# A hybrid decoder trunk on one core: loads of the attention stage issued in smaller pieces and in slots of their own

## The chip, the cores and the metric

The kernel runs on one core of a Trainium2 chip. The metric is the device time of one execution in microseconds (us), taken over several runs; lower is better.

## The reference

Two residual layers over 2048 tokens of width 1024, in float32. The first layer is gated linear attention, the second a dilated sliding-window attention, and both carry a small cross-attention into a memory. The change lies in the second layer:

```python
DIL_GROUPS = ((128, 1), (512, 4), (2048, 16))      # window, dilation
for g, (window, dil) in enumerate(DIL_GROUPS):
    base = g * 3 * MIXER_WIDTH
    qkv = (h @ w_in[:, base:base + 3 * MIXER_WIDTH]).reshape(B, T, 3, DIL_HEADS, DIL_HEAD_DIM)
    q = partial_rope(qkv[:, :, 0], pos)
    k = partial_rope(qkv[:, :, 1], pos)
    o, lse = dilated_group(q, k, qkv[:, :, 2], window, dil)     # blocks of 128 queries, 256 keys
    outs.append(o); lses.append(lse)
wts = jax.nn.softmax(jnp.stack(lses, axis=0), axis=0)
o = jnp.einsum('gbth,gbthd->bthd', wts, jnp.stack(outs, axis=0))
...
branch = jnp.concatenate([o, mem_o], axis=-1) * jax.nn.silu(gate)
x = x + branch @ w_out[i]
```

Six heads of width 128 are computed once for each of three groups. Each head's three outputs are then mixed with softmax weights from the three log-sums, and multiplied by the gate.

## The kernel before

TensorE works in float16 halves: each product is three matmuls (`mm3`, lines 180 to 182: high by high, high by low, low by high).

**The units stage.** `heads` lists 18 units, six heads by the groups 2, 1, 0. The loop at line 1374 runs over 144 slots, `s = 8 n + e`, eight for each unit. A slot does, in this order: the scores of slot s - 10 (`att_scores`), the P·V of slot s - 13 (`att_pv`), and one projection of 512 tokens (`proj_t`): q in even slots, k in odd ones, of the present unit. So a unit's q and k are made while the unit before is still being scored.

- After each q and k pair `evac` (L1171 to L1175) empties PSUM. After every second pair `rope_quad` rotates the first 32 rows: a shuffle (L1181), a product on GpSimd (L1182), a product and a sum on VectorE (L1183, L1184), split halves (L1187 on ScalarE, L1188 on VectorE), and eight copies back into q and k (L1193). The second rotation is wanted by the first scores of its unit.
- `att_scores`: masks and maxima on VectorE (L1223), the statistics (L1227), exponentials on ScalarE (L1232), halves on ScalarE and GpSimd (L173, L174: `ph`), and a DMA transpose from SP (L175: `pt<-ph`) that `att_pv` reads three slots later. `att_pv` copies four blocks of output into `osb`, which goes to memory (`od`).
- `pair_raw` loads a unit's weights, two pieces for q and two for k of 256 KB each, into the one buffer `stg`; `pair_norm` and `pair_split` (L829) scale and split them. `load_v` loads a unit's values, 1 MB, into one of two buffers.
- When a head's three groups are done (x = 0 in the count `h, x = divmod(s - 35, 24)`), `prep_load` loads the log-sums (`nm`, `dn`), and `prep_mix` makes the mixing factors and stores them (`fd<-nm`). Then four quarters y follow, one mix each: `item_og` loads the gate `sg` and three outputs `og`, `item_fb` loads the factors `fb`, spread to all partitions, and `item_mix` forms two products on GpSimd (L1339, L1344), one on VectorE (L1341), two sums (L1347, L1348) and the product with the gate (L1350), and stores it (L1352, `brd<-sg`). `sg`, `og` and `fb` have one buffer each, so a quarter's loads wait for the mix before it. Five heads pass this way in the stage; the sixth is mixed in the tail.

**What sets the order.** Only TensorE runs in program order (`manual_schedule` for PE). The other engines and SP, which issues all DMAs, are ordered by the scheduler when the kernel is built: it places an instruction by its own idea of when its inputs are ready, so program order is a priority and not a slot. At run time each engine then works through its own list strictly in order.

Of the kernel before, what the change touches and what calls it, by code (L numbers as in the profile page):

```python
# [7 lines left out]
F32 = mybir.dt.float32  # L8
F32R = mybir.dt.float32r
F16 = mybir.dt.float16  # L10
# [6 lines left out]
P = 128  # L17
T = 2048
D = 1024
KT = 8  # L20
# [15 lines left out]
def trunk(ctx, tc, a, out):  # L36
    nc = tc.nc
    PE, V, A, G, SY = nc.tensor, nc.vector, nc.scalar, nc.gpsimd, nc.sync
    uid = [0]

    def tl(pool, shape, dt, tag):
        uid[0] += 1
        return pool.tile(shape, dt, name=f"{tag}_{uid[0]}", tag=tag)

    def pool(name, bufs=1, side="left", space=None):
        kw = {"space": space} if space is not None else {"side": side}
        return tc.tile_pool(name=name, bufs=bufs, **kw)
# [10 lines left out]
    stg = ctx.enter_context(pool("stg", 1))  # L58
# [19 lines left out]
    def col(n=1):  # L78
        ncol[0] += n
        return cols[:, ncol[0] - n:ncol[0]]  # L80
# [231 lines left out]
    def neg_of(inv):  # L312
        t = col()
        V.tensor_scalar(out=t, in0=inv, scalar1=-1.0, scalar2=None, op0=ALU.mult)
        return t

    x, w_in_a, w_in_b = a["x"], a["w_in_a"], a["w_in_b"]
# [9 lines left out]
    v_d = {(hp, g, i): tl(dram, [P, 4, 2, 4, P], F16, f"vd{hp}_{g}_{i}") for hp in range(3) for g in range(3)  # L327
           for i in range(2)}
# [26 lines left out]
    with ExitStack() as c1:  # L355
        k1 = c1.enter_context(pool("k1", 2, "right"))
        k2 = c1.enter_context(pool("k2", 1, "right"))
        k0 = c1.enter_context(pool("k0", 1, "right"))
# [223 lines left out]
        for b in range(NB):  # L582
# [28 lines left out]
            if 2 <= b < 7:  # L611
                c0 = 1552 if b == 2 else 1808 + (b - 3) * 256
# [164 lines left out]
    def gdst(t, g, c):  # L777
        if g == 0:
            return t[:, c * 512:(c + 1) * 512]
        f = GROUPS[g][0]  # L780
        n = 512 // f
        return t.rearrange("p (f l) -> p f l", f=f)[:, :, c * n:(c + 1) * n]
# [5 lines left out]
    def wbase(u):  # L788
        return u[1] * 2304 + u[0] * 256

    def pair_raw(c0s):
        raw = tl(stg, [P, KT, 256], F32, "stg")
        for j, c0 in enumerate(c0s):
            v = w_in_b[:, c0:c0 + P].rearrange("(k p) n -> p k n", p=P)
            for k0 in (0, 4):
                SY.dma_start(raw[:, k0:k0 + 4, j * P:(j + 1) * P], v[:, k0:k0 + 4, :])
        return dict(raw=raw, w=[], m=len(c0s))

    def pair_norm(d, cps, common=False):
        raw = d["raw"]  # L800
# [25 lines left out]
    def pair_split(d, j):  # L826
        w, r = d["w"][j], d["raw"][:, :, j * P:(j + 1) * P]
        A.activation(out=w[:, 0], in_=r, func=AF.Copy, scale=d["s"][j])
        V.scalar_tensor_tensor(out=w[:, 1], in0=r, scalar=d["s"][j], in1=w[:, 0], op0=ALU.mult, op1=ALU.subtract)  # L829

    def proj_t(w, c):
        t = mm_bank()
        cs = slice(c * 512, (c + 1) * 512)
        for k in range(KT):
            mm3(t, w[:, 0, k], w[:, 1, k], h2T[:, 0, k, cs], h2T[:, 1, k, cs], k == 0, k == KT - 1)
        return t
# [4 lines left out]
    def head_cols(n):  # L841
        if n == len(heads):
            return GATE2[1:]
        u, i = heads[n]
        return [wbase(u) + i * P, wbase(u) + 768 + i * P]

    with ExitStack() as cv:
# [203 lines left out]
        def memq(c):  # L1051
            for pr in range(2):
                out_q(c, pr, proj_t(wq["w"][pr], c))

        wq = pair_raw([6912, 7040])
        pair_norm(wq, ps_g, True)
        for j in range(2):
# [100 lines left out]
    vp = c4.enter_context(pool("vp", 2))  # L1158
    bk = c4.enter_context(pool("bk", 1))
    qp = c4.enter_context(pool("qp", 2))  # L1160

    def load_v(n):
        u, i = heads[n]
        vt = tl(vp, [P, 4, 2, 4, P], F16, "v")
        SY.dma_start(vt, v_d[u[0], u[1], i])
        return vt

    def evac(ts, c, g, dsts, X):
        r0 = 64 * (c // 2)
        for j in range(2):  # L1170
            A.activation(out=X[r0 + 32 * j:r0 + 32 * j + 32, :], in_=ts[j][0:32, :], func=AF.Copy)  # L1171
        for j in range(2):
            hi = gdst(dsts[j][:, 0, :], g, c)
            A.activation(out=hi, in_=perm(ts[j], g), func=AF.Copy, scale=SQ)
            V.scalar_tensor_tensor(out=gdst(dsts[j][:, 1, :], g, c), in0=perm(ts[j], g), scalar=SQ, in1=hi,  # L1175
                                   op0=ALU.mult, op1=ALU.subtract)

    def rope_quad(c, g, dsts, X):
        cs = slice(c * 512, (c + 1) * 512)
        W = tl(bk, [P, 512], F32, "rw")  # L1180
        V.stream_shuffle(W, X, SWAP)  # L1181
        G.tensor_tensor(out=W, in0=W, in1=rope[1][:, cs], op=ALU.mult)  # L1182
        V.tensor_tensor(out=X, in0=X, in1=rope[0][:, cs], op=ALU.mult)  # L1183
        V.tensor_tensor(out=W, in0=X, in1=W, op=ALU.add)  # L1184
        hl = X.bitcast(F16).rearrange("p (a n) -> p a n", a=2)
        hi, lo = fold(hl[:, 0], g), fold(hl[:, 1], g)
        A.activation(out=hi, in_=perm(W, g), func=AF.Copy, scale=SQ)  # L1187
        V.scalar_tensor_tensor(out=lo, in0=perm(W, g), scalar=SQ, in1=hi, op0=ALU.mult, op1=ALU.subtract)  # L1188
        for y in range(2):
            for j in range(2):  # L1190
                r0 = 64 * y + 32 * j
                for x in range(2):
                    V.tensor_copy(gdst(dsts[j][0:32, x, :], g, c + 2 * y), fold(hl[r0:r0 + 32, x], g))  # L1193
# [124 lines left out]
    def item_og(h, c, osb=None):  # L1318
        cs = slice(c * 512, (c + 1) * 512)
        sg = tl(bk, [P, 512], F32, "sg")  # L1320
        SY.dma_start(sg, sg_d[h][:, cs])
        og = tl(gk, [P, 3, 512], F32, "og")
        if h < 5:
            SY.dma_start(og[:, 0, :], o_d[h][0][:, cs])
        SY.dma_start(og[:, 1, :].rearrange("p (f l) -> p f l", f=4), gdst(o_d[h][1], 1, c))
        SY.dma_start(og[:, 2, :].rearrange("p (f l) -> p f l", f=16), gdst(o_d[h][2], 2, c))
        return h, c, sg, og

    def item_fb(h, c):
        fb = tl(gk, [P, 3, 16, 32], F32, "fb")  # L1330
        src = f_d[h][c, 0, :]
        SY.dma_start(fb.rearrange("p g q l -> p (g q l)"),
                     bass.AP(tensor=src.tensor, offset=src.offset, ap=[[0, P], [1, 1536]]))
        return fb
# [22 lines left out]
    hds, live = {}, {}  # L1357
    wcur, wnext = cur, nxt
# [6 lines left out]
    def scores(at):  # L1365
        att_scores(hds[at // 8], at % 8)

    def pv(at):
        att_pv(hds[at // 8], at % 8)
        if at % 8 == 7 and at // 8 % 3 < 2:  # L1370
            att_stats(hds.pop(at // 8), 0)

    preps, items = {}, {}
    for s in range(NS):
        n, e = divmod(s, 8)
        if s >= 10:
            scores(s - 10)
        if s >= 13:
            pv(s - 13)
        u, i = heads[n]  # L1380
        if e == 0:
            d = wcur
            sc = col()
            V.tensor_scalar(out=sc, in0=d["inv"][0], scalar1=d["inv"][1],
                            scalar2=(128.0 ** -0.5) / (SQ * SQ), op0=ALU.mult, op1=ALU.mult)
            hds[n] = dict(u=u, h=u[0] * 2 + i, sc=sc, nsc=neg_of(sc), pv={}, st={}, osb={},
                          ns=16 if n + 1 < NH else 4, qk=[tl(qp, [P, 2, T], F16, nm) for nm in ("q", "k")])
            if n > 0:
                wnext = pair_raw(head_cols(n + 1))
        c = (0, 2, 1, 3)[e // 2]  # L1390
        live[e % 2] = proj_t(d["w"][e % 2], c)
        if e % 4 == 0:
            rx = tl(bk, [P, 512], F32, "rx")
        if e % 2 == 1:
            evac([live[0], live[1]], c, u[1], hds[n]["qk"], rx)
            wcur = wnext
        if e % 4 == 3:
            rope_quad(c % 2, u[1], hds[n]["qk"], rx)
        if e == 2:
            pair_norm(wcur, ps_tr)  # L1400
        elif 4 <= e < 4 + wcur["m"]:
            pair_split(wcur, e - 4)
        if e == 6:
            hds[n]["v"] = load_v(n)
        h, x = divmod(s - 35, 24)
        if 0 <= h < 5:
            step = 4 if h < 4 else 2
            if x == 0:
                att_stats(hds[3 * h + 2], 0)
                preps[h] = prep_load(h)  # L1410
            if x == 1:
                prep_mix(preps.pop(h))
            y, z = divmod(x - 3 - step, step)
            if 0 <= y < 4 and z == 0:
                item_mix(*items.pop(y))
            y, z = divmod(x - 1 - step, step)
            if 0 <= y < 4 and z == 0:
                items[y] = (item_og(h, y), item_fb(h, y))

    WSH = [P, 4, 256]  # L1420

# [32 lines left out]
    for x in range(14):  # L1454
# [114 lines left out]
        if x in (7, 8, 9, 10):  # L1569
            j, kh = divmod(x - 7, 2)  # L1570
# [9 lines left out]
    for p_ in range(NB):  # L1580
        d = fs.pop(p_)
# [69 lines left out]
```

## Time and profile before

| | |
|---|---|
| runs, median of 3 | 2658.17 us (2656.22 to 2658.51) |
| the profiled execution, its time | 2655.69 us |
| its span, first to last instruction | 2653.7 us |
| mean granted TensorE clock | 0.982 |
| busy: PE, DVE, ACT, POOL | 95%, 61%, 51%, 21% of the span |
| DMA queue of SP | 346.84 MB, 47.6% of 16 engines |

In the profile PE is TensorE, DVE VectorE, ACT ScalarE, POOL GpSimd, SP the queue that issues DMAs. `ps_g` are the banks of scores, `ps_o` and `ps_tr` those of P·V, `ps_mm` and `ps_x` those of projections. A row of a timeline has the start in us, the duration, engine, line, operation, output and inputs, and in brackets how long the engine stood idle before it and what ended that. A transfer in the chain is timed from its issue to its landing. Buffer numbers are left out there, and kept in the orders below.

### The profile page before, as it was taken

The page shows a single profiled execution, that of the slowest core. Times are in us where ns is not written, and L with a number is a line of the kernel's source. Part 1 is how long each engine was busy: PE and PEld are TensorE (multiplying, and loading weights), DVE is VectorE, ACT ScalarE, POOL GpSimd, SP SyncE. Part 2 cuts the span into 40 slices and gives each one's busy share as a digit, 9 for nine tenths or more (in the row PEclk, how much of TensorE's full clock was granted, in tenths as well). Part 3 has the DMA queues.
Part 4 walks back from the last instruction along what each step waited for, and adds up shares of the span by engine and source line. Part 5 has one row for each costly group of instructions (what it writes and reads, how often), then busy time and mean ns, then how long its engine had stood idle before and what let it go on. Part 6 is the DMA issues. An engine that isn't in the chain of part 4 may idle for free.

```text
span 2653.7 us, 45228 instructions
## 1 busy us (share of the span) xinstructions
PE 2524.5 (95%) x17137; PEld 1696.6 (64%) x17137; DVE 1607.6 (61%) x3595; ACT 1343.0 (51%) x2957; POOL 565.5 (21%) x471
## 2 busy tenths in 40 slices
PE   7989999899999999999999999999899998988899
PEld 6879999788889644444444455445454554545798
DVE  7445544656865756556546555766857767577742
ACT  6355544635444446656546455455454554546322
POOL 0000000001211224555442122222322223232200
PEclk9999999999999999999999999999999998999999
DMA  6232111333433445667674244564745547458652
GB/s 207 82 126 98 62 57 70 124 106 104 147 95 95 143 161 138 168 161 187 163 183 143 59 87 104 143 159 108 183 101 146 157 107 184 100 141 216 198 170 87
DMA packets 528493, 349.72 MB, mean 132 GB/s; under 512 B 355650, under 2 KB 467732, under 8 KB 525588
## 3 DMA queue, kind: packets, MB, share of 16 engines
q1 hardware_dynamic: 528276, 346.84, 47.6%
q8 instruction: 134, 2.20, 0.4%
q14 instruction: 83, 0.68, 0.1%
HBM read 185.74 MB, written 95.86 MB: 106 GB/s over the span
## 4 chain that ended last, share of the span: by engine, by line
PE 69%; DMA 9%; DVE 9%; issue 5%; ACT 4%; POOL 2%; SPq 2%; DVEq 0%; ACTq 0%; POOLq 0%
PE ps_mm L180 13%; PE ps_mm L181 13%; PE ps_mm L182 13%; PE ps_x L181 5%; PE ps_x L182 5%; PE ps_x L180 5%; DMA fb<-fd 2%; DMA pt<-ph 1%; PE ps_tr L167 1%; PE ps_o L180 1%; PE ps_o L182 1%; PE ps_o L181 1%; DMA stg<-in_w_in_b 1%; PE ps_g L180 1%; PE ps_g L554 1%
## 5 line engine op out<-in xcount | busy, mean ns | idle before, releaser
L180 PE MATMUL ps_mm<-h2T,w 128*128 128x512 f16 x1112 | 427.3, 384 | 1.8 <-ACT c L947 1.8
L181 PE MATMUL ps_mm<-h2T,w 128*128 128x512 f16 x1112 | 426.4, 383 | 0.0
L182 PE MATMUL ps_mm<-h2T,w 128*128 128x512 f16 x1112 | 425.5, 383 | 0.0
L180 PE MATMUL ps_mm<-w,hT 128*128 128x256 f16 (+1 forms) x1408 | 388.0, 276 | 4.3 <-ACT v L490 1.3
L181 PE MATMUL ps_mm<-w,hT 128*128 128x256 f16 (+1 forms) x1408 | 386.7, 275 | 0.0
L182 PE MATMUL ps_mm<-w,hT 128*128 128x256 f16 (+1 forms) x1408 | 385.5, 275 | 0.4 <-DVE hT L384 0.4
L182 PEld LDWEIGHTS <-w 128*128 128x128 f16 x1952 | 192.3, 99 | 236.1 <-issue 9.1
L181 PEld LDWEIGHTS <-w 128*128 128x128 f16 x1952 | 192.4, 99 | 221.4 <-issue 14.9
L180 PEld LDWEIGHTS <-w 128*128 128x128 f16 x1952 | 192.6, 99 | 214.2 <-issue 7.1
L174 POOL TENSOR_TENSOR ph<-pm,ph 128x512 f16<-128x512 f32 (+2 forms) x144 | 147.2, 1022 | 613.3 <-ACT ph L173 449.3
L1232 ACT ACTIVATE pm<-pm,st,cols 128x256 f32<-128x256 f32 (+1 forms) x288 | 156.4, 544 | 167.1 <-DVE st L1227 166.0
L180 PE MATMUL ps_x<-h2T,w 128*128 128x512 f16 x552 | 210.3, 381 | 3.4 <-ACT h2T L701 2.0
L181 PE MATMUL ps_x<-h2T,w 128*128 128x512 f16 x552 | 210.4, 381 | 1.4 <-DVE h2T L702 1.4
L182 PE MATMUL ps_x<-h2T,w 128*128 128x512 f16 x552 | 210.1, 381 | 0.0
L174 POOL TENSOR_TENSOR stg<-mp,stg 128x512 f16<-128x512 f32 x16 | 18.6, 1159 | 751.7 <-DMA ogd<-og 457.6
L1223 DVE CUSTOM_DVE_ANT_0 pm<-ps_g,mw 128x256 f32<-128x256 f32 (+1 forms) x288 | 93.7, 362 | 101.8 <-PE ps_g L182 100.6
L180 PEld LDWEIGHTS <-hT 128*128 128x128 f16 x1408 | 138.9, 99 | 24.1 <-issue 5.4
L181 PEld LDWEIGHTS <-hT 128*128 128x128 f16 x1408 | 138.9, 99 | 24.0 <-issue 5.7
L182 PEld LDWEIGHTS <-hT 128*128 128x128 f16 x1408 | 139.4, 99 | 18.2 <-DVE hT L384 0.7
L1171 ACT ACTIVATE rx<-ps_mm 32x512 f32<-32x512 f32 x96 | 56.2, 585 | 138.7 <-DVE k L1193 71.1
L181 PE MATMUL ps_g<-k,q 128*128 128x256 f16 (+1 forms) x288 | 70.6, 254 | 15.2 <-DVE k L1193 15.2
L180 PE MATMUL ps_g<-k,q 128*128 128x256 f16 (+1 forms) x288 | 69.0, 253 | 16.4 <-DVE k L1193 16.4
(500 smaller groups left out, 6050.1 us busy)
## 6 DMA issues: line engine op xcount, KB each, us to landing
stg<-in_w_in_b SPq DMA_DIRECT2D x80, 256.0 KB
v<-vd SPq DMA_DIRECT2D x18, 1024.0 KB
fb<-fd SPq DMA_DIRECT2D x24, 768.0 KB
od<-osb SPq DMA_DIRECT2D x68, 256.0 KB
og<-od SPq DMA_DIRECT2D x68, 256.0 KB
x<-in_x SPq DMA_DIRECT2D x32, 512.0 KB
stg<-in_w_in_b SPq DMA_DIRECT2D x24, 512.0 KB
vd<-vo SPq DMA_DIRECT2D x48, 256.0 KB
```

What stands on the lines that cost most here:

```text
L167: PE.transpose(t[:, (k - k0) * P:(k - k0 + 1) * P], src[:, k * P:(k + 1) * P], ident)
L174: G.tensor_tensor(out=lo, in0=src, in1=hi, op=ALU.subtract)
L180: PE.matmul(o, sh, mh, start=first, stop=False)
L181: PE.matmul(o, sh, ml, start=False, stop=False)
L182: PE.matmul(o, sl, mh, start=False, stop=last)
L554: PE.matmul(t[:DK, (h % 2) * DV:(h % 2 + 1) * DV], elb[:, h * DK:(h + 1) * DK], v[:, h * DV:(h + 1) * DV], start=True, stop=True)
L1171: A.activation(out=X[r0 + 32 * j:r0 + 32 * j + 32, :], in_=ts[j][0:32, :], func=AF.Copy)
L1223: V.tensor_tensor_reduce(out=pm[:, at:at + w * P], in0=s[:, at:at + w * P], in1=masks["mw" if w == 2 else "mf"], scale=1.0, scalar=NEG, op ...
L1232: A.activation(out=p_, in_=p_, func=AF.Exp, scale=sc, bias=st[:, jc + jj:jc + jj + 1], accum_out=st[:, ns + jc + jj:ns + jc + jj + 1])
```

## The change

Four things change in the code of the stage. The weight pair's buffer is taken at e = 0 as before, but its two halves are issued at e = 0 and e = 1. The values come in four pieces of 256 KB at e = 4 to 7, not as 1 MB at e = 6. For the first four heads a quarter's outputs are loaded one slot earlier, at x = 4 + 4 y, its factors still at 5 + 4 y, and its mix still stands at 7 + 4 y. For the fifth head the slots stay, with both loads at 3 + 2 y. No arithmetic changes.

```diff
+    def pair_raw(c0s, now=True):
+        d = dict(raw=tl(stg, [P, KT, 256], F32, "stg"), w=[], m=len(c0s), c0=c0s)
+        if now:
+            for j in range(d["m"]):
+                pair_load(d, j)
+        return d
+
+    def pair_load(d, j):
+        v = w_in_b[:, d["c0"][j]:d["c0"][j] + P].rearrange("(k p) n -> p k n", p=P)
+        for k0 in (0, 4):
+            SY.dma_start(d["raw"][:, k0:k0 + 4, j * P:(j + 1) * P], v[:, k0:k0 + 4, :])
...
-    def load_v(n):
+    def load_v(n, x):
         u, i = heads[n]
-        vt = tl(vp, [P, 4, 2, 4, P], F16, "v")
-        SY.dma_start(vt, v_d[u[0], u[1], i])
-        return vt
+        if x == 0:
+            hds[n]["v"] = tl(vp, [P, 4, 2, 4, P], F16, "v")
+        SY.dma_start(hds[n]["v"][:, x], v_d[u[0], u[1], i][:, x])
...
-                wnext = pair_raw(head_cols(n + 1))
+                wnext = pair_raw(head_cols(n + 1), False)
+        if n > 0 and e < wnext["m"]:
+            pair_load(wnext, e)
...
-        if e == 6:
-            hds[n]["v"] = load_v(n)
+        if e > 3:
+            load_v(n, e - 4)
...
-            y, z = divmod(x - 3 - step, step)
-            if 0 <= y < 4 and z == 0:
+            at = [[y for y in range(4) if x == o + step * y] for o in ((4, 5, 7) if h < 4 else (3, 3, 5))]
+            for y in at[2]:
                 item_mix(*items.pop(y))
-            y, z = divmod(x - 1 - step, step)
-            if 0 <= y < 4 and z == 0:
-                items[y] = (item_og(h, y), item_fb(h, y))
+            for y in at[0]:
+                items[y] = [item_og(h, y)]
+            for y in at[1]:
+                items[y].append(item_fb(h, y))
```

What this does to the lists of the engines, at three places of the second cycle (the head h = 1). Lines after 796 are four higher in the new code.

SP, where the log-sums of a finished head are loaded (`nm`, `dn`), before:

```order
L1280 DMA std_57_145<-stT_20112 16x16x8 x2
L1165 DMA v_20308<-vd_1_0_82_170 128x4096
L1293 DMA nm_20116<-std_57_145 16x3x128
L1293 DMA dn_20117<-std_57_145 16x3x128
L1263 DMA od_0_41_129<-osb_20148 128x512
L796 DMA stg_20414<-in_w_in_b 128x4x128 x2
L175 DMA_TRANSPOSE pt_20135<-ph_20134 128x4x128
```

and now:

```order
L1284 DMA std_57_145<-stT_20133 16x16x8 x2
L1170 DMA v_20200<-vd_1_0_82_170 128x1024
L1297 DMA nm_20137<-std_57_145 16x3x128
L1297 DMA dn_20138<-std_57_145 16x3x128
L1267 DMA od_0_41_129<-osb_20169 128x512
L1170 DMA v_20200<-vd_1_0_82_170 128x1024 x2
L175 DMA_TRANSPOSE pt_20156<-ph_20155 128x4x128
L1170 DMA v_20200<-vd_1_0_82_170 128x1024
L801 DMA stg_20444<-in_w_in_b 128x4x128 x4
```

One piece of v stands ahead of `nm` instead of the whole, and the weight loads have moved behind the transpose and the last piece.

VectorE, at the rotation whose copies the next unit's first scores want (`rx`, `rw` are its tiles; `fb`, `og`, `sg` the mix's), before:

```order
L1181 STREAM_SHUFFLE rw_20367<-rx_20176 128x512
L1261 COPY osb_20407<-ps_tr_20329 128x512
L1350 TENSOR_TENSOR sg_20445<-fb_20451,sg_20445 128x16x32
L1175 SCALAR_TENSOR_TENSOR k_19871<-ps_mm_20336,k_19871 128x4x128
L1227 TENSOR_SCALAR st_2803_19963<-mx_20383,cols_88 128x2
L1183 TENSOR_TENSOR rx_20176<-rx_20176,rope_2326_16388 128x512
L1184 TENSOR_TENSOR rw_20367<-rx_20176,rw_20367 128x512
L1188 SCALAR_TENSOR_TENSOR rx_20176<-rw_20367,rx_20176 128x512
```

and now:

```order
L1185 STREAM_SHUFFLE rw_20390<-rx_20197 128x512
L1265 COPY osb_20437<-ps_tr_20352 128x512
L1231 TENSOR_SCALAR st_2803_19984<-mx_20413,cols_88 128x2
L1179 SCALAR_TENSOR_TENSOR k_19892<-ps_mm_20359,k_19892 128x4x128
L1187 TENSOR_TENSOR rx_20197<-rx_20197,rope_2326_16388 128x512
L1345 TENSOR_TENSOR fb_20752<-og_20684,fb_20752 128x512
L1188 TENSOR_TENSOR rw_20390<-rx_20197,rw_20390 128x512
L1351 TENSOR_TENSOR fb_20752<-fb_20752 128x512
L1192 SCALAR_TENSOR_TENSOR rx_20197<-rw_20390,rx_20197 128x512
```

The first mix's last step (L1350) has gone ahead of the shuffle, and the second mix's first product and sum (now L1345, L1351) stand inside the rotation; its second sum stands between the fourth and the fifth copy.

SP, at the transpose of eight blocks that the later of the two waits of TensorE is for, before:

```order
L1352 DMA brd_106_194<-sg_20996 512x1x128
L1165 DMA v_20846<-vd_0_0_80_168 128x4096
L1332 DMA fb_21295<-fd_63_151 128x1536
L175 DMA_TRANSPOSE pt_20601<-ph_20600 128x8x128
L1263 DMA od_2_46_134<-osb_20683 128x512
L1285 DMA std_58_146<-stT_20688 16x128 x2
L796 DMA stg_20965<-in_w_in_b 128x4x128 x4
```

and now:

```order
L1356 DMA brd_106_194<-sg_20957 512x1x128
L1330 DMA og_21247<-od_2_43_131 128x16x32
L1336 DMA fb_21324<-fd_63_151 128x1536
L1325 DMA sg_21245<-sgd_93_181 128x512
L801 DMA stg_20998<-in_w_in_b 128x4x128 x3
L1170 DMA v_20750<-vd_0_0_80_168 128x1024 x3
L1267 DMA od_2_46_134<-osb_20713 128x512
L1289 DMA std_58_146<-stT_20718 16x128 x2
L175 DMA_TRANSPOSE pt_20625<-ph_20624 128x8x128
L1170 DMA v_20750<-vd_0_0_80_168 128x1024
L801 DMA stg_20998<-in_w_in_b 128x4x128
```

The transpose has moved behind the gate's load, three weight loads, three pieces of v, and the stores of `osb` and of the statistics. On GpSimd the fourth mix's two products have moved ahead of the halves (`ph`) that this transpose reads.

More of the change, by code (lines that the diff above doesn't have):

```diff
@@ L789, in wbase @@
         return u[1] * 2304 + u[0] * 256
[L791 to L797, printed above, removed]
+    def pair_raw(c0s, now=True):
[8 more added lines that the diff above has]
+            SY.dma_start(d["raw"][:, k0:k0 + 4, j * P:(j + 1) * P], v[:, k0:k0 + 4, :])
     def pair_norm(d, cps, common=False):
```

## The prediction

> **What bounds the kernel now.** I read the page's chain first (TensorE holds 69% of it), then the waits of TensorE within the units stage, then the time slot by slot.
>
> Who TensorE waited for from 1438 to 2400 us (total, times, longest):
>
> ```profile
> PE ps_o L180 <- DMA pt<-ph: 22.8, 5, 5.7
> PE ps_g L180 <- DVE k L1193: 16.4, 5, 4.4
> PE ps_g L181 <- DVE k L1193: 15.2, 5, 3.5
> ```
>
> Everywhere else in the stage TensorE runs back to back, so only these two places can pay: scores that wait for VectorE's rope copies into k (the rope stall), and P·V that waits for a transpose of probabilities (the transpose stall). Each comes once in 24 slots, where a mixed head passes. Windows of one slot each, from the slot's first scores matmul to the next one's (length, busy times, granted clock, DMA share, GB/s): an undisturbed slot of the first kind and of the second, three of the five rope stalls, all four full transpose stalls, and the fifth cycle's two small ones.
>
> ```profile
> 1549.87:1555.91 6.04, 6.04 (x39) 3.17 (x37) 2.00 (x7) 3.46 (x10) 1.58 (x2) 1.00 0.21 65
> 1568.19:1574.53 6.34, 6.34 (x40) 3.44 (x39) 4.91 (x15) 1.71 (x4) 0.91 (x1) 1.00 1.10 266
> 1699.43:1713.77 14.34, 7.92 (x39) 3.88 (x38) 12.56 (x27) 5.82 (x15) 4.15 (x4) 0.76 0.60 158
> 1865.26:1880.21 14.95, 8.62 (x39) 4.11 (x38) 12.40 (x27) 6.23 (x17) 4.16 (x4) 0.77 0.62 156
> 2360.46:2375.94 15.48, 7.92 (x38) 3.87 (x37) 13.63 (x30) 6.40 (x16) 4.15 (x4) 0.78 0.64 169
> 1732.39:1746.70 14.31, 9.21 (x40) 4.36 (x39) 12.71 (x29) 7.82 (x19) 5.44 (x5) 0.76 1.05 252
> 1898.83:1911.80 12.97, 7.98 (x41) 4.10 (x40) 11.72 (x26) 6.55 (x16) 4.51 (x4) 0.87 1.02 262
> 2062.59:2075.77 13.18, 7.85 (x41) 4.04 (x40) 11.93 (x25) 6.50 (x16) 4.67 (x5) 0.87 1.02 275
> 2227.27:2241.89 14.62, 8.95 (x40) 4.33 (x39) 13.20 (x30) 7.65 (x18) 5.71 (x5) 0.77 0.96 257
> 2394.57:2402.76 8.19, 6.50 (x41) 3.42 (x40) 6.51 (x14) 2.52 (x3) 3.33 (x3) 1.00 1.20 327
> 2402.76:2413.45 10.69, 7.94 (x40) 4.02 (x39) 9.14 (x21) 7.17 (x17) 3.17 (x3) 0.84 0.68 124
> ```
>
> A rope stall costs 14.34 - 6.04 = 8.3, 8.9 and 9.4 us; the four transpose stalls cost 8.0, 6.6, 6.8 and 8.3 over 6.34, together 29.7, mean 7.4. That is more than the waiting: behind it the clock stands at 0.76 to 0.87.
>
> **The rope stall.** VectorE, in its fixed order, holds a mix (L1341 to L1350) ahead of the rope, and the mix waits for its factors fb. Second cycle, VectorE, GpSimd and TensorE (start, duration, in brackets the wait):
>
> ```profile
> 1855.42 2.06 DVE L1341 TENSOR_TENSOR fb<-og,fb 128x512 f32<-128x512 f32 x1 [2.74 <-DMA fb<-fd]
> 1861.71 1.76 DVE L1350 TENSOR_TENSOR sg<-fb,sg 128x512 f32<-128x512 f32 x1
> 1864.89 0.69 DVE L1184 TENSOR_TENSOR rw<-rx,rw 128x512 f32<-128x512 f32 x1
> 1866.83 1.06 DVE L1188 SCALAR_TENSOR_TENSOR rx<-rw,rx 128x512 f16<-128x512 f32 x1 [1.25 <-ACT rx L1187]
> 1868.71 0.29 DVE L1193 COPY k<-rx 32x512 f16<-32x512 f16 x1
> 1869.44 1.19 DVE L1193 COPY q<-rx 32x512 f16<-32x512 f16 x1
> 1869.22 1.26 POOL L1339 TENSOR_TENSOR fb<-og,fb 128x512 f32<-128x512 f32 x1 [2.61 <-DMA fb<-fd]
> 1870.44 1.56 POOL L1344 TENSOR_TENSOR fb<-og,fb 128x512 f32<-128x512 f32 x1
> 1870.64 1.50 DVE L1193 COPY k<-rx 32x512 f16<-32x512 f16 x1
> 1872.20 0.37 PE L181 MATMUL ps_g<-k,q 128*128 128x256 f16 x1 [3.49 <-DVE k L1193]
> ```
>
> What leads there: the values v issued on SP, then three landings from the chain, and one fb of another cycle.
>
> ```profile
> 1832.94 0.39 SPq L1165 DMA_DIRECT2D v<-vd  x1
> 1833.64 5.34 DMA nm<-std
> 1849.40 1.41 DMA fd<-nm
> 1850.96 4.37 DMA fb<-fd
> 2193.61 4.64 DMA fb<-fd
> ```
>
> Part one, values in pieces: the small nm load stands behind 1 MB of v and takes 5.34; the small fd takes 1.41, and fb's 768 KB 4.37, so 768 KB more in front cost 4.37 - 1.41 = 2.96. With one piece of 256 KB ahead, nm lands some 2.9 earlier (bounds 0 and 5.34 - 1.41 = 3.9), and the stabilizer work moves up with it in the new orders of VectorE and ScalarE: the first fb lands at 1855.3 - 2.9 = 1852.4.
>
> Part two, outputs and factors begun apart: the first mix took 1855.3 to 1863.5, 8.1; now its last step stands ahead of the shuffle and the osb copy, 7.6: to 1860.0. Store 0.6, second fb 4.64 (5.29 in a row below): 1865.3. But VectorE now holds the second mix's first product *ahead of L1184*, so the rope waits for that landing. Product 2.0, then as before 1.94 from L1184 to L1188: 1869.2. From L1188 to the end of the k copy it took 1872.14 - 1866.83 = 5.3; copies of 1.19 and 1.50 stood beside GpSimd's two rows there, against 0.29 for their like. Those rows now run under the products (a mask step of VectorE leaves this stretch and a sum of the mix enters it, which is even): 5.3 - 2.1 = 3.2, to 1872.4. So +0.3 per rope stall. Bounds: nm 3.9 sooner and a product of 1.0, -1.7; nm not sooner, the copies still slow and fb at 5.29, 2.9 + 2.1 + 0.7 = 5.7 worse, so +6.0. Times five: +1.5 (-9 to +30).
>
> **The transpose stall.** VectorE's rows around the second and third mix, the third fb's landing, then GpSimd, SP and TensorE:
>
> ```profile
> 1872.79 1.02 DVE L1341 TENSOR_TENSOR fb<-og,fb 128x512 f32<-128x512 f32 x1
> 1875.84 1.39 DVE L1350 TENSOR_TENSOR sg<-fb,sg 128x512 f32<-128x512 f32 x1
> 1879.89 5.29 DMA fb<-fd
> 1885.28 1.02 DVE L1341 TENSOR_TENSOR fb<-og,fb 128x512 f32<-128x512 f32 x1 [3.44 <-DMA fb<-fd]
> 1891.55 1.34 POOL L174 TENSOR_TENSOR ph<-pm,ph 128x512 f16<-128x512 f32 x1 [2.67 <-ACT ph L173]
> 1893.86 0.55 SPq L1352 DMA_DIRECT2D brd<-sg  x1
> 1894.51 1.14 SPq L1165 DMA_DIRECT2D v<-vd  x1
> 1895.70 0.42 SPq L1332 DMA_DIRECT2D fb<-fd  x1
> 1896.18 2.49 SPq L175 DMA_TRANSPOSE pt<-ph  x1
> 1904.48 0.27 PE L180 MATMUL ps_o<-pt,v 128*128 128x128 f16 x1 [4.99 <-DMA pt<-ph]
> ```
>
> The probabilities are ready at 1892.9, SP waits till 1893.86 with the store of the third mix, and then 1 MB of v and 768 KB of fb go just ahead of the transpose: 8.3 from issue to use. After: the second mix ends some 2.6 behind the k copy instead of 5.1, at 1875.0; store 0.6, third fb 5.29: 1880.9 instead of 1885.2. Its four VectorE steps now stand together (the second mix took 4.4 like that; 5.2 taken, as GpSimd starts with it): 1886.1, so the store goes 7.8 earlier. Behind it og and the fourth fb, landed at 1892.8. GpSimd's two products come ahead of the probabilities: 1892.8 + 1.26 + 1.56 + 1.34 = 1897.0. SP has three weight loads, three v pieces, the osb store and two statistics stores ahead; osb waits behind the fourth product on VectorE (2.06, then masks, shuffle and copy, together about 4.1, an estimate), and three stores at 0.55 take 1.6: the transpose is issued at 1898.5. The 1.5 MB of pieces behind fb drain by 1892.8 + 5.9 = 1898.7, and 256 KB take 1.41 + 2.96 / 3 = 2.4 (an estimate): landed 1901.0. TensorE asks at 1899.5 + 0.3, so 1.2 of stall instead of 4.99 (bounds 0, and 7 if the transpose again takes 8.3). The fifth cycle's 1.69 wait cost its slot 1.85 at clock 1.00; I take 1.3: 7.4 - 1.3 = 6.1, times four: -24.5 (-30 to +8). The fifth cycle keeps 1 MB of w_out ahead of its transpose: 0 (-6 to +3).
>
> Weight pairs in two: in both orders the four loads stand slots ahead of their place in the program, since the buffer is free after the split; the pieces of v now go ahead of them. Their reader, the next norm on ScalarE, has no wait in front of TensorE in the first fence: 0, with TensorE's own work as the cover; without it, one load more ahead of the norm, 1.0.
>
> Clock: the 10.69 slot lost 1.6 beyond its 2.75 of waiting at clock 0.84, so a short wait can cost clock too. [...]
>
> **Sum.** +1.5 - 24.5 + 0 = -23. The profiled execution took 2655.69 (span 2653.7 and 2.0 around it), 2.5 below the median 2658.17, so 2632.7 there and 2635 as a median.
>
> **Rivals.**
> - *The rope stall grows.* The second fb now stands in front of the rope. Each us that it lands later than 1865.3 costs five. Against a gain of 24.5 it decides from 4.9 + 0.3 late; at the bound of 6.0, with the clock's half again as in the slots above, +36 - 24 = +12: 2670. For it: VectorE waited 36.3 us for fb already, and now four mixes wait each time instead of two. Against: the chain starts 2.9 earlier.
>
> ```profile
> DVE fb L1341 <- DMA fb<-fd: 36.3, 10, 4.8
> ```
>
> - *The pieces cost what they save.* If each piece pays fd's 1.41 by itself, three pieces more ahead of the transpose land it 4.2 later: stall 5.4, as before; with the rope's +1.5, 2660. Or the change hardly acts, since the scheduler had the loads early anyway: the same number. [...] No row before shows v in pieces.
> - *Both stalls shrink*, if the fb of the first mix comes 3.9 earlier and the copies run free: the five rope stalls lose about 7 of their 8 to 9 us each: 2658 - 24.5 - 35 = 2598.
>
> **Chances.** Forecast (2622 to 2650) 0.47; rope grows 0.22; pieces cost or nothing acts 0.16; both shrink 0.15. Two executions differ by about 0.2%, 5 us, which no measurement of this kernel tells from nothing. Faster 0.62, same 0.16, slower 0.22. The range leaves out a third of the last case and of the first rival: 2606 to 2672.
>
> **What would show it.** Right: the transpose waits of TensorE fall from 22.8 to under 10, the k waits stay near 31; VectorE's waits for fb come up to 20 times and grow past 36 us; nm lands in under 3.5. Wrong: k waits over 40, or a wait for v or stg on TensorE's side; or a transpose that still takes 8 from issue to landing.

## The result, and the profile after

The changed kernel takes 2665.85 us (median of 7 runs, 2664.74 to 2674.15), the kernel before 2658.27 (7 runs beside them, 2656.22 to 2659.79). The ratio is 1.0037, 95% interval 1.0026 to 1.0048: slower by 0.37%, some 8 us, where 23 us of gain were forecast. The profiled execution of the changed kernel took 2665.85 us, with a span of 2664.0.

Lines behind the edits are numbered four or five higher now: the mix's products are L1343, L1345 and L1348 and its gate step L1354, the rope's sum L1188, its low half L1192, its copies L1197.

Who TensorE waited for from 1438 to 2410 us (total, times, longest), after:

```profile
PE ps_g L180 <- DVE k L1197: 35.2, 5, 7.7
PE ps_o L180 <- DMA pt<-ph: 21.3, 4, 5.8
PE ps_g L181 <- DVE k L1197: 7.2, 5, 1.5
```

The waits for k rose from 31.6 to 42.4 us; those for the transpose went from 22.8 to 21.3 only. Three rope slots and the four transpose slots in the columns of the prediction's windows:

```profile
1700.21:1717.10 16.89, 8.26 (x38) 3.97 (x37) 12.87 (x27) 6.40 (x15) 5.69 (x4) 0.70 0.69 174
1868.75:1884.88 16.13, 7.74 (x38) 3.83 (x37) 12.88 (x27) 5.91 (x14) 5.70 (x4) 0.79 0.69 171
2372.02:2389.22 17.20, 8.56 (x38) 4.02 (x37) 13.40 (x28) 6.54 (x15) 6.07 (x5) 0.70 0.68 177
1735.72:1750.18 14.46, 9.40 (x40) 4.39 (x39) 9.30 (x26) 6.96 (x17) 5.65 (x4) 0.76 0.79 147
1903.50:1918.08 14.58, 8.77 (x40) 4.25 (x39) 10.07 (x28) 7.20 (x18) 6.22 (x5) 0.77 0.71 167
2073.16:2086.11 12.95, 8.02 (x41) 4.09 (x40) 9.11 (x25) 6.31 (x16) 4.87 (x3) 0.87 0.72 162
2240.00:2253.46 13.46, 7.92 (x41) 4.03 (x39) 9.62 (x27) 6.52 (x17) 5.39 (x4) 0.87 0.77 196
```

Over undisturbed slots of 6.04 us, the five rope slots lose 54.6 us, against 42.5 before. The transpose slots, with the two behind each counted in, lose 30.1 against 29.7. So two things need a cause: why the rope stall grew by 2.4 us a time, and why the transpose stall kept its size although its old reason is gone.

**The rope.** VectorE, GpSimd and TensorE in the second cycle, from the first mix's end:

```profile
1862.70 1.08 DVE L1354 TENSOR_TENSOR sg<-fb,sg 128x512 f32<-128x512 f32 x1
1869.53 1.01 DVE L1345 TENSOR_TENSOR fb<-og,fb 128x512 f32<-128x512 f32 x1 [1.92 <-DMA fb<-fd]
1869.60 2.03 POOL L1343 TENSOR_TENSOR fb<-og,fb 128x512 f32<-128x512 f32 x1 [3.20 <-DMA fb<-fd]
1870.46 1.72 DVE L1188 TENSOR_TENSOR rw<-rx,rw 128x512 f32<-128x512 f32 x1
1871.59 1.96 POOL L1348 TENSOR_TENSOR fb<-og,fb 128x512 f32<-128x512 f32 x1
1872.10 2.00 DVE L1351 TENSOR_TENSOR fb<-fb 128x512 f32<-128x512 f32 x1
1874.02 1.44 DVE L1192 SCALAR_TENSOR_TENSOR rx<-rw,rx 128x512 f16<-128x512 f32 x1
1876.02 0.37 PE L180 MATMUL ps_g<-k,q 128*128 128x256 f16 x1 [6.94 <-DVE k L1197]
1877.50 0.28 DVE L1197 COPY k<-rx 32x512 f16<-32x512 f16 x1
1877.84 0.37 PE L181 MATMUL ps_g<-k,q 128*128 128x256 f16 x1 [1.45 <-DVE k L1197]
1878.11 0.28 DVE L1197 COPY k<-rx 32x512 f16<-32x512 f16 x1
```

The rope's sum L1188 (0.69 before) takes 1.72 and its low half (1.06) 1.44 while GpSimd's two products run. The copies, at 0.28, now run free. From the second factors' landing to the last copy it is 1878.39 - 1869.53 = 8.86 us, and 8.86 or 8.87 in each of the five cycles. TensorE's second wait ends at the third of the four copies into k, 8.25 us after the landing.

**The transpose.** SP, ScalarE, GpSimd and TensorE in the same cycle:

```profile
1893.20 1.38 SPq L1336 DMA_DIRECT2D fb<-fd  x1
1896.67 0.63 ACT L173 ACTIVATE ph<-pm 128x512 f16<-128x512 f32 x1
1900.69 2.05 POOL L1343 TENSOR_TENSOR fb<-og,fb 128x512 f32<-128x512 f32 x1 [10.45 <-DMA fb<-fd]
1902.69 1.53 POOL L1348 TENSOR_TENSOR fb<-og,fb 128x512 f32<-128x512 f32 x1
1904.19 2.98 POOL L174 TENSOR_TENSOR ph<-pm,ph 128x512 f16<-128x512 f32 x1
1907.19 1.25 SPq L175 DMA_TRANSPOSE pt<-ph  x1
1909.97 0.27 PE L180 MATMUL ps_o<-pt,v 128*128 128x128 f16 x1 [5.81 <-DMA pt<-ph]
```

The old reason was 8.3 us from issue to use, behind 1 MB of values and 768 KB of factors; now it is 1909.97 - 1907.19 = 2.8. But GpSimd's half of the probabilities, for which ScalarE's half was ready at 1897.30, starts at 1904.19: it stands behind the fourth mix's two products, and the fourth factors land 7.4 us after their issue.

### The profile page after: what moved, and what is told of

Read it like the earlier page. It is cut to its first block, busy times and chain, and to the rows that moved or that the text cites. A ratio compares the mean times of both kernels' runs of the same rounds, so it can differ in the third digit from the quotient of the medians.

```text
span 2664.0 us, 45293 instructions
## 1 busy us (share of the span) xinstructions
PE 2524.9 (95%) x17137; PEld 1695.3 (64%) x17137; DVE 1590.8 (60%) x3595; ACT 1345.7 (51%) x2957; POOL 585.2 (22%) x471
## 5 line engine op out<-in xcount | busy, mean ns | idle before, releaser
L174 POOL TENSOR_TENSOR ph<-pm,ph 128x512 f16<-128x512 f32 (+2 forms) x144 | 157.2, 1091 | 594.2 <-ACT ph L173 418.1
L180 PE MATMUL ps_g<-k,q 128*128 128x256 f16 (+1 forms) x288 | 68.4, 251 | 35.2 <-DVE k L1197 35.2
L173 ACT ACTIVATE ph<-pm 128x512 f16<-128x512 f32 (+2 forms) x144 | 76.9, 534 | 3.7
```

The source lines that it names most:

```text
L173: A.activation(out=hi, in_=src, func=AF.Copy)
L174: G.tensor_tensor(out=lo, in0=src, in1=hi, op=ALU.subtract)
L180: PE.matmul(o, sh, mh, start=first, stop=False)
```

## The experiments

The profiled executions reach the units stage anywhere between 1500 and 1512 us. So, beside the medians and ratios to the kernel before (from runs beside each other), this table gives the profiled stage by itself: what the five rope slots lose over 6.04 us each, what the four transpose slots and the two behind each lose over 6.34, the time of the other 126 slots (rest), and that of all 143 (stage). Each of these four columns comes from a single execution.

| kernel | median us | ratio, 95% | rope | transpose | rest | stage |
|---|---|---|---|---|---|---|
| before | 2658.27 | | 42.5 | 29.7 | 777 | 955.5 |
| after | 2665.85 | 1.0037 (1.0026 to 1.0048) | 54.6 | 30.1 | 773 | 964.4 |
| pieces only | 2668.07 | 1.0029 (1.0017 to 1.0041) | 58.9 | 25.2 | 776 | 966.7 |
| slots only | 2660.33 | 0.9996 (0.9985 to 1.0007) | 45.1 | 28.3 | 779 | 958.3 |
| 4th mix on VectorE | 2657.98 | 0.9991 (0.9982 to 1.0001) | 57.1 | 17.1 | 775 | 955.3 |
| 4th mix late | 2656.85 | 0.9994 (0.9985 to 1.0003) | 56.1 | 7.1 | 781 | 950.6 |
| 2nd mix on VectorE | 2642.88 (one run) | | 57.7 | 2.6 | 774 | 940.6 |
| 2nd mix behind the rope | 2653.42 | 0.9970 (0.9959 to 0.9981) | 33.9 | 29.8 | 779 | 949.1 |
| 2nd to 4th late | 2644.84 | 0.9952 (0.9937 to 0.9967) | 34.3 | 0.0 | 803 | 943.8 |
| 1st mix behind the rope | 2660.11 | 1.0000 (0.9990 to 1.0010) | 0.0 | 42.2 | 809 | 957.7 |
| the same, whole values | 2633.16 | 0.9898 (0.9883 to 0.9913) | 0.0 | 39.9 | 785 | 930.7 |
| 1st behind, rest late | 2624.58 | 0.9880 (0.9864 to 0.9896) | 10.9 | 0.0 | 807 | 924.6 |
| the same, fifth cycle too | 2621.89 | 0.9870 (0.9855 to 0.9885) | 0.0 | 0.0 | 813 | 919.0 |
| the same, whole values | 2625.91 | 0.9890 (0.9872 to 0.9907) | 0.0 | 4.3 | 811 | 921.5 |

### Which part acts

Pieces alone: of the change's diff the lines on `load_v` and its call, and none of the others.

> Only the values in four pieces; weight pairs, outputs and factors begun as before. Theory A (the engines' new lists are the whole of the change, and the pieces alone make them): as the full change, 2666 us (2662 to 2670), TensorE's waits for k some 42 us in the units stage and for the transposed probabilities some 21. Rival B (the earlier outputs and factors carry part of the loss): between the two kernels, 2660 to 2663, with waits for k of 32 to 38.

Slots alone: the lines on `pair_raw` and `pair_load` and on the table `at`, with `load_v` left as before.

> The other two parts without the pieces: weight pairs in two, outputs and factors begun in slots of their own, values in one load. Theory A: no change, 2658 us (within 0.1% of the kernel before), waits for k 31 to 32, for the transposes 22 to 23. Rival B: 2661 us or more, since the second factors then stand in front of the rope here too.

The first measures as the full change, the second as the kernel before (intervals 1.0017 to 1.0041 and 0.9985 to 1.0007); B is out. The order of the instructions in the traces says why: with the pieces alone VectorE, ScalarE, GpSimd and SP have the same instructions in the same order as in the full change, with the slots alone as before. The scheduler places the other loads by readiness, and their places in the program don't move them. The full change is the four pieces of values and the lists that the scheduler makes of them. These two pairs also show how much the stage's columns vary for the same lists: up to 4.9 us at the rope or the transpose, 2.8 in the whole stage. Smaller differences in one column show nothing.

### The transpose: the fourth mix in GpSimd's list

The fourth mix's two products of GpSimd on VectorE:

```diff
-        G.tensor_tensor(out=fb[:, 2], in0=og[:, 2, :]...
+        (V if c == 3 else G).tensor_tensor(out=fb[:, 2], in0=og[:, 2, :]...
```

and the same for `f1v`.

> The changed kernel, with the fourth mix's two products of GpSimd on VectorE, so that the probabilities do not stand behind them in GpSimd's list and the transpose is issued after one piece of values instead of three. Theory A (the late transpose is the wait of GpSimd's products for the fourth factors): waits for the transposes fall from 21 us to under 6, waits for k stay at 40 to 45; four slots lose 1 us instead of 7.5, 2666 - 26 = 2640 us (2634 to 2650). Rival C (the DMA backlog of weight loads and value pieces holds the transpose as it did before): waits for the transposes 16 us or more, 2660 to 2668 us.

Waits for the transposes fell from 21.3 to 11.4 us, and the time to 2657.98, both between the two theories: 3.6 us are left at the old place and 7.8 came up at the next pair.

```profile
PE ps_tr L180 <- DMA pt<-ph: 7.8, 4, 3.0
PE ps_o L180 <- DMA pt<-ph: 3.6, 5, 1.4
```

That moves the products and SP's list at once. The cleaner test leaves the products on GpSimd and lets the fourth mix wait for a rope that comes after the transpose, by a small VectorE step that adds 0 times three columns of k to the outputs:

```diff
-                item_mix(*items.pop(y))
+                it = items.pop(y)
+                if y == 3 and h < 4:
+                    o3 = it[0][3][0:32, :, 0:1]
+                    rc = 3 * 512 // GROUPS[heads[n - 1][0][1]][0]
+                    kl = hds[n - 1]["qk"][1][0:32, 1, rc:rc + 3].rearrange("p (a b) -> p a b", b=1)
+                    V.scalar_tensor_tensor(out=o3, in0=kl, scalar=0.0, in1=o3, op0=ALU.mult, op1=ALU.add)
+                item_mix(*it)
```

> The changed kernel, with the fourth mix alone, in the first four cycles, waiting for a rope after the transpose. The three other mixes, the fourth factors' load and the rope stall stay as in the changed kernel; in GpSimd's list the probabilities no longer stand behind the fourth products. Theory A (that place in GpSimd's list is what holds the transpose): waits for the transposes fall from 21 us to under 4, waits for k stay at 40 to 45: 2666 - 26 = 2640 us (2634 to 2648). Rival C (the transfers ahead, 768 KB of factors, three weight loads and a piece of values, hold it): waits for the transposes 10 us or more, 2652 us or more.

TensorE's waits, and GpSimd and SP at the second cycle's transpose:

```profile
PE ps_g L180 <- DVE k L1197: 38.9, 9, 7.8
PE ps_g L181 <- DVE k L1197: 10.8, 9, 1.5
PE ps_o L180 <- DMA pt<-ph: 4.7, 3, 2.1
PE ps_tr L180 <- DMA pt<-ph: 1.2, 1, 1.2
...
1896.57 1.67 SPq L1336 DMA_DIRECT2D fb<-fd  x1
1900.34 1.49 SPq L801 DMA_DIRECT2D stg<-in_w_in_b  x3
1901.92 0.45 SPq L1170 DMA_DIRECT2D v<-vd  x1
1902.41 2.35 SPq L175 DMA_TRANSPOSE pt<-ph  x1
...
1900.75 1.16 POOL L174 TENSOR_TENSOR ph<-pm,ph 128x512 f16<-128x512 f32 x1 [7.13 <-ACT ph L173]
```

The waits for transposes fall to 5.9 us (A wanted under 4, C 10 or more), with 768 KB of factors, three weight loads and a piece of values still issued just ahead; in this cycle TensorE doesn't wait at all. That is theory A in kind, and C is out. The slots lose 23.0 us less, near the 26 expected, but the stage as a whole gets only 13.8 shorter: 7.7 come back in the rest of it (waits for k came 9 times, not 5, and rose to 49.7 where 40 to 45 were expected), and 1.5 in the rope slots. So the total missed its range of 2634 to 2648.

### The rope: the second mix, GpSimd beside it, and the first mix

The same small step for the second mix, on the last copy of the rope that stalls:

```diff
-                if y == 3 and h < 4:
+                if y == 1 and h < 4:
```

> The changed kernel, with the second mix of each of the first four cycles made to wait for the rope's last copy into k (a step of three columns that adds 0 times k to the outputs). In the lists the fourth mix then also falls behind the transpose. Theory A (the second mix inside the rope is what the rope stall costs): k is ready 7.4 us sooner, waits for k fall from 42 us to under 15, four of the five rope slots lose 2 us instead of 10.9; the transposes, free of the fourth mix, keep up: 2666 - 36 - 20 = 2610 us (2595 to 2630). Rival D (the stall only moves: TensorE arrives 9 us sooner at a transpose that comes no sooner): waits for k fall, waits for the transposes rise by as much, 2650 to 2666 us. Rival E (the first mix sets the rope, as in the kernel before): waits for k stay over 28, 2650 us or more.

VectorE in the second cycle; the rope's sum, low half and last copy:

```profile
1866.69 0.69 DVE L1188 TENSOR_TENSOR rw<-rx,rw 128x512 f32<-128x512 f32 x1
1868.58 1.05 DVE L1192 SCALAR_TENSOR_TENSOR rx<-rw,rx 128x512 f16<-128x512 f32 x1 [1.20 <-ACT rx L1191]
1871.66 0.28 DVE L1197 COPY k<-rx 32x512 f16<-32x512 f16 x1
```

The rope slots lose 20.7 us less, the waits for k fall to 22.1. Theory A was right in direction only: it wanted under 15. What is left is 4.3 to 6.8 us in each of the four slots; the test with the first mix below shows whose it is, so E holds in part. And D holds in part: its total, 2650 to 2666, came true, and with the fourth mix out of the way the transposes lose 29.8 us still. Now the *third* mix's store is late in SP's list. The probabilities were there at 1895.54; SP could issue that store only at 1896.47, and two pieces go ahead of the transpose as well, which then takes 5.4 us from issue to use, not 2.8:

```profile
1894.20 1.34 POOL L174 TENSOR_TENSOR ph<-pm,ph 128x512 f16<-128x512 f32 x1 [2.68 <-ACT ph L173]
1896.47 0.89 SPq L1356 DMA_DIRECT2D brd<-sg  x1
1897.45 1.07 SPq L1170 DMA_DIRECT2D v<-vd  x2
1898.57 1.26 SPq L175 DMA_TRANSPOSE pt<-ph  x1
1903.93 0.26 PE L180 MATMUL ps_o<-pt,v 128*128 128x128 f16 x1 [5.04 <-DMA pt<-ph]
```

The second mix waiting for the next unit's last rope instead, so that second, third and fourth leave this place:

```diff
+            at[2] = [y for y in range(4) if x == (12 if y == 1 and h < 4 else (7 if h < 4 else 5) + step * y)]
-                    kl = hds[n - 1]["qk"][1]...
+                    kl = hds[n]["qk"][1]...
```

> The changed kernel, with the second mix of the first four cycles waiting for the next head's last rope copy, some eight slots later; third and fourth follow it. Around the transpose that waits there is then no mix, no factors and no store. Theory A (the transpose is held by a mix's store and products in the lists of SP and GpSimd): waits for that transpose under 4 us in all, waits for k some 22 as with the second mix just behind the rope, 2653 - 26 = 2627 us (2615 to 2640). Rival D (the stall only moves: the fourth mix now stands between the steps of a later rope in VectorE's list): a new wait for k of 15 us or more at that rope, 2645 us or more.

The transpose slots lose nothing now (0.0 against 29.8), so it was a mix that held them. Whether its store, its products or its loads did, this run doesn't separate, since all of them left. But the rest of the stage takes 803 instead of 779 us, at slots that had run free: 24 of 30 came back. Rival D was right that the stall moves, and wrong about where: waits for k rose only from 22.1 to 27.0, while waits for transposes in later slots came to 11.9. The total, 2644.84, lies outside A's range.

GpSimd beside the rope, tested by itself: the second mix's two products on VectorE.

```diff
-        (V if c == 3 else G).tensor_tensor(...
+        (V if c == 1 else G).tensor_tensor(...
```

> The changed kernel, with the second mix's two GpSimd products on VectorE; they stand with the third product ahead of the rope's sum. In the changed kernel it is 8.86 us from the landing of the second factors to the end of the copies into k, with the rope's sum at 1.71, the mix's sum at 2.00 and the rope's low half at 1.44. Theory A (these are slow because GpSimd's products run beside them): 0.7, 0.7 and 1.05, so that two more products of 1.0 are paid for by what the three save, 8 to 9 us in all. Rival H (they are slow by themselves, or by the transfers): durations as before, 10.5 us or more.

```profile
1863.61 0.69 DVE L1343 TENSOR_TENSOR fb<-og,fb 128x512 f32<-128x512 f32 x1 [2.20 <-DMA fb<-fd]
1864.22 1.00 DVE L1345 TENSOR_TENSOR fb<-og,fb 128x512 f32<-128x512 f32 x1
1865.14 1.05 DVE L1348 TENSOR_TENSOR fb<-og,fb 128x512 f32<-128x512 f32 x1
1866.11 0.68 DVE L1188 TENSOR_TENSOR rw<-rx,rw 128x512 f32<-128x512 f32 x1
1866.71 0.68 DVE L1351 TENSOR_TENSOR fb<-fb 128x512 f32<-128x512 f32 x1
1868.33 1.04 DVE L1192 SCALAR_TENSOR_TENSOR rx<-rw,rx 128x512 f16<-128x512 f32 x1
1872.48 0.28 DVE L1197 COPY k<-rx 32x512 f16<-32x512 f16 x1
```

0.68, 0.68 and 1.04 where the changed kernel has 1.72, 2.00 and 1.44: theory A. From landing to last copy it is 9.15 us, with two more products, the gate step and mask steps in it, so the stall itself doesn't shrink. What I hadn't expected: the scheduler now puts the probabilities ahead of the fourth products, and the transpose slots lose 2.6 us instead of 30.1. In this one execution that is worth more than the rope, and it agrees with the fourth-mix test.

The first mix behind that rope, in all five cycles, with pieces and with whole values:

```diff
-                if y == 1 and h < 4:
+                if y == 0:
```

> The changed kernel, with the first mix of every cycle waiting for the rope's last copy into k, so that no mix stands ahead of that rope; the other mixes follow as the lists put them, the second one's store just ahead of the transpose. Theory A (what is left of the rope stall, 34 us of slot losses after the second mix was moved, is the first mix): waits for k under 5 us, rope slots lose under 1 us each; TensorE comes some 5 us sooner to the transpose, whose slots lose 7 to 10 instead of 7.5: 2653 - 34 + 6 = 2625 us (2615 to 2640). Rival D: all of it turns up at the transpose, 2648 us or more. Rival F (the rope is late by itself, with evacuation and shuffle of its own head): waits for k stay over 15.

> As the kernel with the first mix behind the rope, but with the values in one load of 1 MB and the weights in one: the mixes stand alike in VectorE's list, so what differs is the pieces themselves. In SP's list the transpose that waits stands behind 1 MB of values and the third factors. Theory A (pieces act through the order and through what lies ahead of the transpose): waits for k under 5, waits for the transposes longer than with pieces by 2 to 4 us each: 8 to 16 us slower than the kernel with pieces. Rival G (the pieces are dearer in themselves, each with a start-up of its own): the kernel with whole values is as fast as that with pieces, or faster.

Both lose nothing at the rope: F is out, and the whole rope stall is the mixes standing ahead of it. With pieces everything comes back elsewhere, as D said: 42.2 at the transposes and 809 in the rest. With whole values the transposes lose 39.9, but the rest is 785, and the kernel is 1% faster than with pieces, where theory A had it 8 to 16 us slower. This need not be the price of pieces: SP's lists differ too. In the second cycle with pieces the third factors stand behind the transpose (issued at 1892.10) and five more loads: they are issued at 1898.29, their products on GpSimd start at 1904.74, and a later transpose's probabilities, for which ScalarE's half is ready at 1907.73, start behind them at 1908.14. With whole values the third factors go out just behind the values at 1878.94, ahead of the transpose at 1879.44, and the products start at 1886.39. So the pair doesn't decide G.

Both moves together (the first mix on `hds[n - 1]`, the second on `hds[n]`), first in four cycles, then in all five, and that with whole values:

```diff
-                if y == 1 and h < 4:
+                if y < 2 and h < 4:                    # first
+                if y == 0 or y == 1 and h < 4:         # second and third
```

> Both: the first mix behind that rope, the second to fourth behind the next head's last rope, in the first four cycles. Theory A: waits for k of the fifth cycle alone (8 to 10 us), waits for the transposes under 4: 2653 - 22 - 26 = 2605 us (2595 to 2625). Rival D: a new wait at the later rope behind the fourth mix, 2630 us or more.

> As the kernel with the first mix behind the rope and the others behind the next head's rope, and the fifth cycle's first mix now also behind its rope. Theory A: the fifth rope slot, which lost 10.9 us, loses under 2; nothing else changes: 2624 - 9 = 2615 us (2608 to 2624). Rival D: the fifth cycle's later mixes and its transpose give it back, 2622 us or more.

> The same placing of the mixes, with the values in one load and the weights in one. The mixes now stand in the same places of VectorE's and GpSimd's lists as with pieces, so the difference is the pieces alone. Theory A (no cost of their own, they only let other transfers through sooner): within 0.2% of the kernel with pieces, 2615 us, or slower by up to 10 through the transpose that stands behind 1 MB. Rival G (the pieces are dearer in themselves): faster than with pieces by 5 us or more.

The first, 2624.58 us, lies at the upper end of A's range, since with the mixes late the rest of the stage takes some 30 us more; waits for the transposes came to 13.8 us, in later slots, not under 4. The second, 2621.89, is in its range too, though D's bound of 2622 is as near; of the fifth rope slot's 10.9 us the stage keeps 5.6, the rest comes back behind it. The intervals of the two overlap (0.9864 to 0.9896, 0.9855 to 0.9885), so the time alone doesn't show this step. With the mixes in the same places of the lists, whole values and pieces have overlapping intervals too (0.9872 to 0.9907, 0.9855 to 0.9885): no price of the pieces themselves can be measured, and G is out there. The best version, 2621.89 us, is 1.3% faster than the kernel before.

## Why the prediction was wrong

The forecast was +1.5 at the rope and -24.5 at the transpose; the slots show +12.1 and +0.4. Here are its steps in the second cycle, on the clock of the kernel before. The changed kernel reaches that rope slot 3.49 us later (1868.75 against 1865.26), so its times are less 3.49.

| step | predicted | measured |
|---|---|---|
| first factors land | 1852.4 | 1853.5 |
| first mix ends | 1860.0 | 1860.3 |
| second factors land | 1865.3 | 1866.0 |
| third copy into k ends | 1872.4 | 1874.3 |
| second mix ends | 1875.0 | 1876.4 |
| third factors land | 1880.9 | 1881.8 |
| third mix ends | 1886.1 | 1888.4 |
| fourth factors land | 1892.8 | 1897.1 |
| probabilities done | 1897.0 | 1903.7 |
| transpose issued | 1898.5 | 1903.7 |
| TensorE reads it | 1901.0 | 1906.5 |

- *Pieces let the small load through.* Right: nm was issued at 1837.67 and used at 1840.04, 2.4 us, under the 3.5 asked. The first factors lost over a third of the 2.9 again, mostly since a transpose of probabilities stands between the stores of `fd` (issued until 1850.12) and their load (1852.15) in SP's list.
- *The second mix ahead of the rope, +0.3 a time.* The place was right, the size wrong: +2.4 in the mean of the five slots (1.2 to 4.3), 2.2 of it waiting for k. In the second cycle the copy that TensorE waits for ends 1.9 later than predicted. 0.7 of that is the later landing. The rest is the stretch from landing to that copy, put at 2.0 + 1.94 + 3.2 = 7.1 and measured at 0.93 + 3.56 + 3.76 = 8.25. The step that failed is the middle term, "then as before 1.94 from L1184 to L1188". The new order has a sum of the mix (now L1351) in that place, which the prediction put at nothing; and that sum and the rope's took 2.00 and 1.72 beside GpSimd's products, against some 0.7 without them. I had given this slow-down to the product alone, which took 1.01. The copies did get free of GpSimd, as predicted, and the sum that enters among them (L1352, 0.69) was nearly even, as it said.
- *The transpose.* Its first half was right: with the big loads ahead of it issued 6.7 us earlier, instead of 1.75 MB just before, it takes 2.8 us from issue to use, not 8. The second half failed at "GpSimd's two products come ahead of the probabilities: 1892.8 + 1.26 + 1.56 + 1.34". I saw the wait that this place makes, and undersized it: the fourth factors took 7.4 from issue, not 5.29, and the three GpSimd rows 2.05, 1.53 and 2.98. With the third mix's 6.5 instead of 5.2, and its factors 0.9 late, that is 2.1 + 2.4 + 1.3 + 0.9 = 6.7 us at the probabilities, more than the 6.1 of gain that each slot was to bring. The test with the fourth mix late shows what the transposes lose without this step: 7 us in place of 30, which is 22.6 less than before, near the forecast 24.5.
- *The rivals.* "The rope stall grows" came near with its 2670 by luck: the second factors were 0.7 late, not 4.9, and it was not needed that they be later, because the transpose brought nothing to set against. That is the error of the chances: its price was reckoned on top of a gain taken as safe, though the gain hung on one place in GpSimd's list. Two of its sums were also off: with 1.5 already lost it decides from 4.9 - 0.3, not + 0.3, and five times 6.0 is 30, so 36 holds a fifth for the clock and not a half. "The pieces cost what they save" named a stall of 5.4, and 5.81 was measured, but not for its reason: the transpose took 2.8 from issue to use.
- *The signs.* Waits for k over 40, a sign of being wrong: reached, 42.4. Waits for the transposes under 10: missed, 21.3. VectorE's waits for factors up to 20 times and past 36 us: right, 19 times and 55.9.

```profile
DVE fb L1345 <- DMA fb<-fd: 55.9, 19, 5.6
```

## What to carry to other kernels

A scheduler that places work by readiness can turn a change of transfer sizes into a new order on every engine: read the order first, then price each wait at the head of a list with all that stands behind it. When a long wait is explained by a backlog, look for what comes last once the backlog is gone; here a load that was off the path became the head of GpSimd's list, and 30 us stayed 30 us. Work that nobody waits for (the mixes) should stand behind the work that TensorE waits for, and moving only part of it moves the stall to the next place. Even the best order here gives part back: its stalls are gone from both places, and the rest of the stage takes 813 us where it took 777.

## What the runs showed of the hardware

- Beside each other, either VectorE or GpSimd took longer in these runs. VectorE's 128x512 float32 sum took 0.69 with GpSimd idle (at 1864.89 in the kernel before) and 1.72 to 2.00 beside a GpSimd product. At 1904.19 it was the other way: GpSimd's 128x512 step took 2.98 (1.15 at 1917.61 of the same kernel, with VectorE idle) while VectorE ran three steps at 0.67. In the rope of the changed kernel each of the two slow sums ended 0.55 us after the GpSimd product beside it (1872.18 after 1871.63, 1874.10 after 1873.55), and the slow GpSimd step ended 1.03 us after the last of the three VectorE steps. What makes one of them the slow one, no run here shows.
- In these runs a short wait came with a lower clock in some slots and not in others. Slots of TensorE with their length, busy times, clock, DMA share and GB/s: first of the kernel with the second mix behind the rope (2.31 us of waiting, in pieces of 1.38 and 0.93), then of that with the fourth mix late (one wait of 2.12), with the second to fourth late (11.04 - 8.34 = 2.70 in which TensorE isn't busy), and with the first behind and the rest late (10.44 - 6.82 = 3.62):

```profile
1868.48:1878.83 10.35, 8.04 (x38) 3.64 (x37) 9.41 (x20) 3.68 (x10) 4.34 (x3) 0.84 0.33 82
...
2233.89:2242.51 8.62, 6.50 (x40) 3.44 (x39) 4.88 (x15) 4.58 (x11) 0.92 (x1) 1.00 1.03 213
...
2266.52:2277.56 11.04, 8.34 (x40) 3.99 (x39) 10.80 (x19) 3.50 (x8) 5.59 (x3) 0.85 0.80 201
...
2094.40:2104.84 10.44, 6.82 (x40) 3.56 (x39) 9.09 (x16) 3.69 (x8) 5.99 (x3) 1.00 0.80 187
```

The first loses 2.0 us beyond its waits over the undisturbed 6.04, at clock 0.84, the second 0.2 over 6.34, at clock 1.00. The last two stand at 0.85 and 1.00, though the fourth has more idle time than the third. So in these slots neither the longest wait (1.38 at clock 0.84, 2.12 at 1.00) nor the idle time in a slot (2.70 at 0.85, 3.62 at 1.00) parts those that lose clock from those that don't. What does, no run here shows.
